# Hybrid decoder layer: norm chain, order and held splits between the output projection and the FFN, order of attention tiles, and a new table of weave distances

## The chip, the cores and the metric

The kernel runs on one core of a Trainium2 chip. The metric is the device time of one execution in microseconds (us), the median over several runs. In the profile PE is TensorE's matmul stream, PEld its weight loads, DVE is VectorE, ACT is ScalarE, POOL is GpSimd and SP is SyncE, which here only issues DMAs (SPq). The granted TensorE clock is 1.00 at full speed and 0.50 at half.

## The reference, cut to what matters

One layer on 1024 tokens of width 1024, in float32:

```python
h = rms_norm(x, norm_mix_pre)
z = h @ w_in                            # q, k, v of attention; r, k, v and low-rank columns of RWKV-7
attn = rms_norm(dilated_attention(q, k, v), attn_out_gain)
rw = rwkv7(...)                         # 8 heads, state 64x64, a recurrence over the tokens
mixed = concat([attn, rw], -1) @ w_out
x = x + rms_norm(mixed, norm_mix_post)
h = rms_norm(x, norm_ffn_pre)
f = square(relu(h @ w_ffn_up)) @ w_ffn_down
x = x + rms_norm(f, norm_ffn_post)
# rms_norm(x, g) = x * rsqrt(mean(x*x) + 1e-6) * g
```

## The kernel before, in words

Every large product is made of three matmuls (`mm3`, L59): each operand is split into a high part (fp32r, an ACT copy) and a low part (DVE: value minus high part), and high x high, low x high and high x low are added up in PSUM. So each operand costs one ACT and one DVE instruction before PE can use it.

**The weave (to about 435 us).** The input projection is cut into slabs of 128 columns; each slab is 2 x 8 filler pieces of three matmuls. Between them the RWKV work is woven in by a planner, `drive`. It has a list of jobs, each a generator that issues some instructions and then yields the PE time it took and the time until its next step may come. The planner keeps its own clock: it takes the first job in the list that is due, adds its PE time, and if none is due it takes one filler piece (0.7). The due times stand in the table `WAIT` (L31): `'ab1.0'` is the time after the first step of job `ab1`, `'e0'` the time before job `e0` starts, and keys such as `PE7`, `EO7_0`, `VU7`, `T7` and `H7` times after particular marks. Inside the planner PE and SP keep this written order; ACT and DVE are ordered by Tile's scheduler by priority. For each unit n of 128 tokens there are the jobs `ld` (its loads AR and K), `zl` (its load Zp), `vu`, `ab` (products with a mask; T1, T2 come out), `e` (E, from Zp and T2), `c` (the recurrence: `c.0` and `c.2` multiply T1 with HV, `c.1` and `c.3` T2 with VU) and `g` (gate, norm, store). T2 lies in two tiles TR0 and TR1 for even and odd units. The slabs aq3, ak3 and av3 come after the last unit; 28 of their pieces are issued ahead of the attention (`LEAD`).

**Attention.** `at_load` (L869 to L880) loads for a pair of heads the tiles qs, kh and kl of each head, 12 DMAs on SP, and `at_s`, `at_t` and `at_v` make scores, transposes and outputs. These tiles lie in a pool that is opened over the space of pools closed before: places are handed out in the order in which the tiles are created, and a load into a place waits until the last user of what lay there is through.

**Output projection to FFN (about 610 to 730 us).** For tiles of 128 tokens in the order 0, 4, 1, 5, 2, 6, 3, 7 `half_mm` (L1002) multiplies half of the mixed row with half of `w_out`: 24 matmuls into two PSUM banks `pm`. `mix_x1` (L1009 to L1037) makes both norms and the residual of one tile on ACT and DVE: squares of pm, the root (`rstd1`, L97 to L106), y = pm * rstd * gain (L1028), y + x (L1029), the store to `x_d`, a square of y (L1032), the second root, and the scaled tile `yg` (L1035 on DVE, L1036 on ACT). `mix_h2` (L1039) transposes `yg` on PE and makes from it, for token half 0, high and low parts HB and raw copies, and for half 1 the combinations T1 to T4. From here PE's order is the order in which the program is written.

The FFN's two products are done with a Strassen-like scheme of seven products on halves. Up: for each of 16 groups j, `up_first` (L1218) makes two products X and Y from a split weight W1, `first_out` evacuates them, and `up_last` makes five more (X with T2, Z with T1, X with T3, Z with HB, X with T4) from the splits W2, W3 and W4 of `up_rest` (L1197). Before the last tile was ready, groups 0 and 1 had their `up_first`; group 2 had it directly after the last tile's transposes. `split_w` (L1185 to L1190) is the split of a weight. The results are spilled to DRAM (`u_d`), and the down product reads them back. The last norm, `final` (L1408), uses `rstd1` too.

`rstd1` was: ACT root s of the mean, DVE v = -mean/2, y = 1/s, then a Newton step, y * (1.5 + v * y * y), in three steps.

Of the kernel before, what the change touches and what calls it, by code (L numbers as in the profile page):

```python
# [1 line left out]

# [38 lines left out]
def hybrid_kernel(tc, x, par, cst, strip, win, wup_lora, gup, gnwb, grow, wout, wup, wdown, out, dbg=None):  # L41
# [22 lines left out]
    with (  # L64
# [10 lines left out]
        eps = cp.tile([P, 32], F32, name="eps")[:, 0:1]  # L75
# [18 lines left out]
        eps1 = cp.tile([P, 1], F32, name="eps1")  # L94
        A.activation(eps1, eps, AF.Sqrt)

        def rstd1(y, ssum, nm, more=eps, more_v=-0.5 * NORM_EPS):  # L97
# [6 lines left out]
            V.tensor_tensor(m, y, y, OP.mult)  # L104
            V.tensor_tensor(m, m, v_, OP.mult)
            V.scalar_tensor_tensor(y, m, 1.5, y, OP.add, OP.mult)  # L106
# [762 lines left out]
        def at_load(p):  # L869

            at[p] = QS, KH, KL = [], [], []
            for h in range(2):
                hs_ = slice(64 * h, 64 * h + 64)
                for L, nm, q, js in ((QS, "qs", p, (0, 1)), (KH, "kh", 4 + p, (0, 0)), (KL, "kl", 4 + p, (1, 1))):
                    t = aset[p % 2].tile([P, S], F32R, name=f"{nm}{p}_{h}", tag=f"{nm}{h}", bufs=1)
                    for d in range(2):
                        nc.sync.dma_start(t[own[d]].bitcast(F32), qk_d[q, js[d], hs_, :])
# [124 lines left out]
        def half_mm(t, pm, mx, k0, first, last):  # L1002
            for n in range(2):
                ns = slice(n * 512, n * 512 + 512)
                for k in range(4):
                    w = WO[k0 + k]
                    mm3(pm[n], mx[:, 0, k], mx[:, 1, k], w[:, 0, ns], w[:, 1, ns], first and k == 0, last and k == 3)

        def mix_x1(t, pm, y=None):  # L1009
# [12 lines left out]
            for n in range(2):  # L1022
                A.activation(jm, src[n], AF.Square, accum_out=st[:, 2 + n:3 + n])
            V.tensor_tensor(st[:, 2:3], st[:, 2:3], st[:, 3:4], OP.add)
            rstd1(st[:, 4:5], st[:, 2:3], f"m{t}")
            for n in range(2):
                ns = slice(n * 512, n * 512 + 512)
                V.scalar_tensor_tensor(y[:, ns], src[n], st[:, 4:5], gpM[:, ns], OP.mult, OP.mult)  # L1028
# [6 lines left out]
            V.tensor_tensor(yg, y, gF, OP.mult)  # L1035
            A.activation(yg, yg, AF.Copy, scale=st[:, 6:7])  # L1036
            return yg  # L1037

        def mix_h2(t, yg, between=None):  # L1039
# [9 lines left out]
            for q in range(h, 2):  # L1049
                A.activation(HB[q, h][:, 0, :, qs], pt[q], AF.Copy)  # L1050
            if h == 0:
                for q in range(2):
                    A.activation(f((T3, T4)[q]), pt[q], AF.Copy)
                    last = V.tensor_tensor(HB[q, 0][:, 1, :, qs], pt[q], HB[q, 0].bitcast(F32)[:, 0, :, qs], OP.subtract)  # L1054
                return last
# [105 lines left out]
        pms[1] = pm_new(ORD[1], "bc")  # L1161
        for i in range(8):
# [21 lines left out]

        def split_w(raw, nm, E=V, pool=None):  # L1185
# [3 lines left out]
            E.tensor_tensor(w[:, 1, 0:n], raw, w[:, 0, 0:n].bitcast(F32), OP.subtract)  # L1189
# [7 lines left out]
        def up_rest(j, r1, r2):  # L1197
# [340 lines left out]
```

## Time and profile before

| what | value |
|---|---|
| median of 3 runs | 1333.93 us (1330.68 to 1336.93) |
| the profiled execution's own time | 1336.02 us |
| its span, first to last instruction | 1334.2 us |
| mean granted TensorE clock | 0.987 |
| DVE busy | 900.3 us, 67% |
| ACT busy | 629.0 us, 47% |
| POOL busy | 40.9 us, 3% |
| DMA | 240.57 MB, mean 180 GB/s |
| chain that ended last, by engine | PE 68%, DVE 12%, DMA 11%, ACT 5% |

The span is what the trace shows of one execution; the execution's own time is 1.8 us longer. Lines such as L1036 are lines of the kernel before. A row of the timeline has start, length, engine, line, operation, output and inputs, shapes and a count; in brackets stands the idle time before it on its engine and what ended it. Matmuls overlap, so the start of the next one tells more than the length. Most matmuls have L47, the helper `mm`, and are told apart by their tiles.

### The profile page before, as it was taken

To read this page: it belongs to the slowest core of one execution; us is meant where nothing else is said; L and a number is where in the kernel's file an instruction comes from. 1 tells how busy PE (TensorE), PEld (TensorE's weight loads), DVE (VectorE), ACT (ScalarE), POOL (GpSimd) and SP (SyncE) were. 2 spreads that over 40 slices of the span, in tenths; PEclk is the share of its full clock that TensorE was granted. 3 is DMA by queue.
4 is the path that set the end of the run, shared out by engine and by line. 5 is a ranking of instruction groups with operands and counts; after the bars stand their busy time and mean duration, and the time that the engine had idled before them with its cause. 6 is when DMAs were issued, how large, how long until landed. Compare 5 with 4: busy or idle time off the path is not lost.

```text
span 1334.2 us, 23879 instructions
## 1 busy us (share of the span) xinstructions
PE 1268.8 (95%) x9488; PEld 1043.3 (78%) x9488; DVE 900.3 (67%) x1648; ACT 629.0 (47%) x1033; POOL 40.9 (3%) x59
## 2 busy tenths in 40 slices
PE   6899999999988979999998999999999999999997
PEld 5678788877776867787887888888887888888885
DVE  7877678542878456555878977766766776446585
ACT  7653423232554267665746444444444444444343
POOL 0000000000000000000000000000000002000211
PEclk9999999999998989999999999999999999999998
DMA  7345767976684687403523554444457984345564
GB/s 260 112 181 158 208 156 204 279 206 193 215 264 130 200 234 199 127 25 96 174 103 118 195 169 150 138 146 174 150 195 244 369 300 147 95 142 198 194 214 151
DMA packets 168240, 240.57 MB, mean 180 GB/s; under 512 B 56672, under 2 KB 93792, under 8 KB 168128
## 3 DMA queue, kind: packets, MB, share of 16 engines
q1 hardware_dynamic: 158784, 213.86, 50.5%
q10 hardware_dynamic: 8064, 20.98, 4.8%
q0 software_dynamic: 1280, 4.20, 0.8%
q8 instruction: 75, 1.23, 0.4%
q14 instruction: 37, 0.30, 0.1%
HBM read 161.90 MB, written 77.09 MB: 179 GB/s over the span
## 4 chain that ended last, share of the span: by engine, by line
PE 68%; DVE 12%; DMA 11%; ACT 5%; issue 3%; SPq 1%; DVEq 0%; ACTq 0%
PE X L47 13%; PE dX L47 9%; PE Z L47 7%; PE pm L47 6%; PE dZ L47 5%; PE Y L47 3%; PE dY L47 3%; PE z_v L47 3%; PE z_aq L47 3%; PE z_ak L47 2%; PE pS L47 2%; PE po L47 2%; PE pT L920 2%; PE O L47 2%; PE z_r L47 1%
## 5 line engine op out<-in xcount | busy, mean ns | idle before, releaser
L47 PE MATMUL dX<-wow,wou 128*128 128x512 f32 x768 | 178.2, 393 | 2.8 <-DVE wow L1189 1.6
L47 PEld LDWEIGHTS dX<-wow,wou 128*128 128x128 f32 x768 | 144.8, 189 | 35.5 <-DVE wow L1189 3.5
L47 PE MATMUL dZ<-wow,wou 128*128 128x512 f32 x384 | 87.4, 389 | 0.0
L1188 ACT ACTIVATE wow<-wd 128x1024 fp32r<-128x1024 f32 x40 | 42.3, 1060 | 89.1 <-PE dZ L47 29.7
L47 PEld LDWEIGHTS dZ<-wow,wou 128*128 128x128 f32 x384 | 72.1, 188 | 14.9
L1189 DVE TENSOR_TENSOR wou<-ur,wou 128x1024 fp32r<-128x1024 f32 x56 | 71.7, 1282 | 9.1 <-ACT wou L1188 8.9
L1189 DVE TENSOR_TENSOR wow<-wd,wow 128x1024 fp32r<-128x1024 f32 x40 | 49.2, 1231 | 35.6 <-ACT wow L1188 35.2
L1188 ACT ACTIVATE wou<-ur 128x1024 fp32r<-128x1024 f32 x56 | 58.5, 1048 | 21.1 <-DMA ur<-u_d 13.8
L908 DVE CUSTOM_DVE_ANT_0 S<-pS,stripT 128x512 f32<-128x512 f32 (+3 forms) x64 | 37.7, 589 | 39.2 <-PE pS L47 37.6
L910 ACT ACTIVATE S<-S,mn 128x128 f32<-128x128 f32 (+7 forms) x64 | 49.3, 771 | 16.2 <-DVE mn L908 15.7
L1276 ACT ACTIVATE r<-u 128x512 f32<-128x512 f32 x48 | 30.0, 626 | 48.4 <-DVE u L1274 48.2
L920 PE MATMUL pT<-cst,S 128*128 128x128 f32 x288 | 44.4, 281 | 7.6 <-ACT PT L922 6.3
L47 PE MATMUL pm<-WO,mxr 128*128 128x512 f32 x192 | 49.2, 400 | 0.8 <-DVE mxr L988 0.8
L47 PE MATMUL X<-HB,wo 128*128 128x512 f32 x180 | 45.2, 401 | 3.9 <-DVE HB L1054 2.3
L1189 DVE TENSOR_TENSOR wow<-TK,wow 128x1024 fp32r<-128x1024 f32 x16 | 20.8, 1301 | 38.9 <-ACT wow L1188 38.9
L47 PE MATMUL Z<-HB,wo 128*128 128x512 f32 x192 | 46.1, 389 | 0.0
L47 PE MATMUL z_aq<-hT,wh_aq 128*128 128x512 f32 x128 | 46.1, 421 | 0.0
L1460 POOL TENSOR_TENSOR E<-E,gpF 128x512 f32<-128x512 f32 x12 | 21.1, 1771 | 806.3 <-DMA xf<-x_d 640.3
L47 PE MATMUL pm<-WO,mxa 128*128 128x512 f32 x192 | 45.7, 393 | 0.0
L47 PE MATMUL z_av<-hT,wh_av 128*128 128x512 f32 x128 | 44.9, 408 | 0.0
L920 PEld LDWEIGHTS pT<-cst,S 128*128 128x128 f32 x288 | 32.9, 142 | 15.3 <-ACT PT L922 11.3
L47 PE MATMUL z_k<-hT,wh_k 128*128 128x512 f32 x128 | 43.4, 396 | 1.4 <-DVE z L234 1.4
(394 smaller groups left out, 3060.7 us busy)
## 6 DMA issues: line engine op xcount, KB each, us to landing
ur<-u_d SPq DMA_DIRECT2D x56, 512.0 KB, 4.2
wd<-in_wdown_dram SPq DMA_DIRECT2D x40, 512.0 KB, 4.4
u_d<-S SPq DMA_DIRECT2D x64, 256.0 KB, 2.1
u_d<-u SPq DMA_DIRECT2D x48, 256.0 KB, 2.3
wr_upa<-in_wup_dram SPq DMA_DIRECT2D x16, 512.0 KB, 3.6
wr_upb<-in_wup_dram SPq DMA_DIRECT2D x16, 512.0 KB, 4.1
TK<-in_wdown_dram SPq DMA_DIRECT2D x16, 512.0 KB, 6.8
x<-in_x_dram SPq DMA_DIRECT2D x8, 512.0 KB, 7.1
```

What stands on the lines that cost most here:

```text
L47: return PE.matmul(o, lhsT, rhs, start=start, stop=stop, skip_group_check=True)
L908: V.tensor_tensor_reduce(Sx[:, lo:hi], pS[:, :hi - lo], stripT[:, so:so + hi - lo], 1.0, 3e38 if k == 0 else mn[:, 0:1], OP.add, OP.min, a ...
L910: A.activation(Sx[:, :w], Sx[:, :w], AF.Exp, scale=-1.0, bias=mn[:, nbk - 1:nbk], accum_out=at[p, "den"][:, i, h:h + 1])
L920: PE.transpose(pt[:, j], Sx[:, (4 * k + j) * P:(4 * k + j + 1) * P], ident)
L1188: A.activation(w[:, 0, 0:n], raw, AF.Copy)
L1189: E.tensor_tensor(w[:, 1, 0:n], raw, w[:, 0, 0:n].bitcast(F32), OP.subtract)
L1276: A.activation(r, src, AF.Relu)
L1460: G.tensor_tensor(e, e, gn[n], OP.mult)
```

## The change

- `rstd1` takes another last step (Heron): with s the root of mean/4 on ACT and v = mean/4, y = 1/(s + v/s). For one column that is a reciprocal, one fused step and a reciprocal; for two columns four steps.
- `mix_x1` multiplies pm with the gain right after the squares, without waiting for the root. After the root one fused step per half makes y * rstd + x, and ACT squares each half as it comes. The last scaling is halved between ACT and DVE.
- The transposes of tile 3 (`ORD[6]`) go into the last `half_mm`, ahead of its last six matmuls.
- Splits are held back by `issue_after`: the second early split W1[1] behind the high and low parts of tile 3, the splits of groups 2 and 3, W2 of group 0 and the T splits behind the last tile's squares and sums; some of the last tile's combinations behind W2's low part; W3 and W4 of group 0 behind T1's low part.
- Groups 2 and 3 (before: group 2) have their `up_first` before group 0's `up_last`; Y2 moves from bank w to bank a. Group 3's split lies in the tiles of `mixy`, which is closed later.
- `at_load` creates the tiles of the second head first. The order of the loads stays.
- `WAIT` has 147 entries that are new, changed or gone.

```diff
-WAIT = {..., 'mrg0.0': 31.5, 'e0': 14.5, 'ab1.0': 2, 'c1.2': 2, 'c2.0': 0, 'e3': 0, 'ab4.0': 3.5, 'c6.0': 0, 'c7.0': 8.0, 'H7': 6.0, 'PE7': 2.5, ...}
+WAIT = {..., 'mrg0.0': 28.0, 'e0': 14.0, 'ab1.0': 8, 'c1.2': 1, 'c2.0': 0.5, 'e3': 1.5, 'ab4.0': 0, 'c6.0': 0.5, 'c7.0': 2.5, 'H7': 2.5, 'PE7': 0, ...}
...
-            A.activation(sq_, ssum, AF.Sqrt, scale=1.0 / D, bias=more)
-            V.tensor_scalar(v_, ssum, -0.5 / D, more_v, op0=OP.mult, op1=OP.add)
-            V.reciprocal(y, sq_)
-            V.tensor_tensor(m, y, y, OP.mult)
-            V.tensor_tensor(m, m, v_, OP.mult)
-            V.scalar_tensor_tensor(y, m, 1.5, y, OP.add, OP.mult)
+            A.activation(sq_, ssum, AF.Sqrt, scale=0.25 / D, bias=more)
+            V.tensor_scalar(v_, ssum, 0.25 / D, more_v, op0=OP.mult, op1=OP.add)
+            V.reciprocal(m, sq_)
+            if n == 1:
+                V.scalar_tensor_tensor(m, m, v_, sq_, OP.mult, OP.add)
+            else:
+                V.tensor_tensor(m, m, v_, OP.mult)
+                V.tensor_tensor(m, m, sq_, OP.add)
+            V.reciprocal(y, m)
...
-            at[p] = QS, KH, KL = [], [], []
+            T = {(nm, h): aset[p % 2].tile([P, S], F32R, name=f"{nm}{p}_{h}", tag=f"{nm}{h}", bufs=1) for h in (1, 0) for nm in ("qs", "kh", "kl")}
...
+        BK = 2
...
+                    if between and (n, k) == (1, BK):
+                        between()
...
+            for n in range(2):
+                V.tensor_tensor(y[:, hs[n]], src[n], gpM[:, hs[n]], OP.mult)
             V.tensor_tensor(st[:, 2:3], st[:, 2:3], st[:, 3:4], OP.add)
             rstd1(st[:, 4:5], st[:, 2:3], f"m{t}")
...
-                V.scalar_tensor_tensor(y[:, ns], src[n], st[:, 4:5], gpM[:, ns], OP.mult, OP.mult)
-            V.tensor_tensor(y, y, xt, OP.add)
+                ld = V.scalar_tensor_tensor(y[:, hs[n]], y[:, hs[n]], st[:, 4:5], xt[:, hs[n]], OP.mult, OP.add)
+                la = A.activation(jh[:, hs[n]], y[:, hs[n]], AF.Square, accum_out=st[:, (5, 7)[n]:(6, 8)[n]])
...
-            A.activation(yg, yg, AF.Copy, scale=st[:, 6:7])
+            A.activation(yg[:, hs[0]], yg[:, hs[0]], AF.Copy, scale=st[:, 6:7])
+            V.tensor_scalar(yg[:, hs[1]], yg[:, hs[1]], st[:, 6:7], None, op0=OP.mult)
...
-            half_mm(ORD[i], pms[i], ax.pop(i), 0, i < 2, True)
+            half_mm(ORD[i], pms[i], ax.pop(i), 0, i < 2, True, last_h0 if i == 7 else None)
...
-        for j in range(2):
-            W1[j] = split_w(up_raw(2 * j, f"e{j}"), f"1_{j}")
-        h6 = mix_h2(ORD[6], ygs.pop(6))
+        W1[0] = split_w(up_raw(0, "e0"), "1_0")
+        with tc.issue_after(h6s[0][0].ins), tc.issue_after(h6s[0][1].ins):
+            W1[1] = split_w(up_raw(2, "e1"), "1_1")
...
+        with tc.issue_after(ea.ins), tc.issue_after(ed.ins):
+            W1[2] = [stg.tile([P, D], F32R, name=f"w12{q}", tag=("wh", "wl")[q]) for q in range(2)]
...
+            W1[3] = [M["yp"].tile([P, D], F32R, name=f"w13{q}", tag="y") for q in range(2)]
...
+            ws0 = up_rest(0, up_raw(0, "a0"), up_raw(1, "b0"), True)
+            for k, v in TS.items():
+                A.activation(v[1][:, :, early_], v[0][:, :, early_], AF.Copy)
...
+            for j in (2, 3):
+                with tc.high_priority(offset=20):
+                    c11s[j - 2] = first_out(j - 2)
+                up_first(j, W1[j])
...
-                elif j < 3:
+                elif j < 4:
```

More of the change, by code (lines that the diff above doesn't have):

```diff
@@ L1 @@
+import contextlib
 import math
+import contextlib
 import numpy as np
@@ L1000, in half_a, with half_mm @@
             return half_t(t, m, "a", tag)
-        def half_mm(t, pm, mx, k0, first, last):
+        BK = 2
+        MX = {}
+        def half_mm(t, pm, mx, k0, first, last, between=None):
             for n in range(2):
@@ L1049, in mix_h2 @@
             for q in range(h, 2):
-                A.activation(HB[q, h][:, 0, :, qs], pt[q], AF.Copy)
+                la = A.activation(HB[q, h][:, 0, :, qs], pt[q], AF.Copy)
             if h == 0:
                 for q in range(2):
-                    A.activation(f((T3, T4)[q]), pt[q], AF.Copy)
                     last = V.tensor_tensor(HB[q, 0][:, 1, :, qs], pt[q], HB[q, 0].bitcast(F32)[:, 0, :, qs], OP.subtract)
-                return last
+                with tc.issue_after(la.ins):
+                    for q in range(2):
+                        A.activation(f((T3, T4)[q]), pt[q], AF.Copy)
+                return la, last
             V.tensor_tensor(f(T1), pt[0], f(T3), OP.subtract)
@@ L1059, in mix_h2 @@
                 between()
-            V.tensor_tensor(HB[1, 1][:, 1, :, qs], pt[1], HB[1, 1].bitcast(F32)[:, 0, :, qs], OP.subtract)
-            V.tensor_tensor(f(T3), f(T2), f(T3), OP.subtract)
-            V.tensor_tensor(f(T4), f(T4), f(T2), OP.subtract)
+            with (tc.issue_after(W2I[0].ins) if between else contextlib.nullcontext()):
+                V.tensor_tensor(HB[1, 1][:, 1, :, qs], pt[1], HB[1, 1].bitcast(F32)[:, 0, :, qs], OP.subtract)
+                V.tensor_tensor(f(T3), f(T2), f(T3), OP.subtract)
+                V.tensor_tensor(f(T4), f(T4), f(T2), OP.subtract)
         def pm_new(t, tags):
@@ L1188, in split_w @@
             A.activation(w[:, 0, 0:n], raw, AF.Copy)
-            E.tensor_tensor(w[:, 1, 0:n], raw, w[:, 0, 0:n].bitcast(F32), OP.subtract)
+            low = E.tensor_tensor(w[:, 1, 0:n], raw, w[:, 0, 0:n].bitcast(F32), OP.subtract)
+            if nm == "2_0":
+                W2I.append(low)
             return w
@@ L1221, in up_first @@
             prod(XB[j], op2(w, 0), HQ[0, 0], True)
-            y = bank(f"Y{j}", "w" if j == 2 else YT[j % 2])
+            y = bank(f"Y{j}", YT[j % 2])
             prod(y, op2(w, 1), HQ[1, 0], True)
@@ L1255, in t2_late @@
             t_low(2, late, V)
-        mix_h2(ORD[7], ygs.pop(7), t2_late)
-        up_first(2, W1[2])
-        for k in (1, 3, 4):
-            A.activation(TS[k][1][:, :, late], TS[k][0][:, :, late], AF.Copy)
-            new_low(k)
-            t_low(k, slice(0, 512), V)
-        HT = {k: v[1:] for k, v in TS.items()}
+        with tc.high_priority(offset=PRI[0]):
+            mix_h2(ORD[7], ygs.pop(7), t2_late)
         mix_ctx.__exit__(None, None, None)
-        M["yc"].__exit__(None, None, None)
         if "x1" in dbg:
@@ L1314, in up_last @@
                     spill(i, j, t)
-            c11s = {j: first_out(j) for j in range(2)}
+            c11s = {}
+            for j in (2, 3):
+                with tc.high_priority(offset=20):
+                    c11s[j - 2] = first_out(j - 2)
+                up_first(j, W1[j])
+            for k in (1, 3, 4):
+                A.activation(TS[k][1][:, :, late], TS[k][0][:, :, late], AF.Copy)
+                new_low(k)
+                if k == 1:
+                    with tc.high_priority(offset=PRI[1]):
+                        t1l = t_low(k, slice(0, 512), V)
+                    with tc.issue_after(t1l.ins):
+                        ws0 = ws0()
+                else:
+                    t_low(k, slice(0, 512), V)
+            HT = {k: v[1:] for k, v in TS.items()}
             for j in range(NPR):
```

75 lines of the change are left out of this document (43 added, 32 removed).

## The prediction

> **What bounds the kernel now.** I read the page first, then the busy time by stretches, then PE's timeline with the waits in brackets, then ACT, DVE and the DMA queue of SP around those waits. The first two lines are the page's; the others are stretches: PE busy, PEld busy, DVE busy, ACT busy, POOL busy, then the granted TensorE clock, DMA share and GB/s.
>
> ```profile
> span 1334.2 us, 23879 instructions
> PE 1268.8 (95%) x9488; PEld 1043.3 (78%) x9488; DVE 900.3 (67%) x1648; ACT 629.0 (47%) x1033; POOL 40.9 (3%) x59
> 750.00:800.00 50.00, 50.00 (x222) 41.44 (x221) 40.22 (x59) 21.83 (x32) 0.00 (x0) 1.00 0.54 188
> 316.60:320.00 3.40, 3.40 (x16) 2.23 (x12) 0.00 (x0) 1.19 (x2) 0.00 (x0) 0.50 0.89 169
> 425.80:435.50 9.70, 7.40 (x113) 6.61 (x109) 7.08 (x20) 2.87 (x5) 0.00 (x0) 0.50 0.19 65
> 435.50:439.50 4.00, 4.00 (x12) 3.14 (x11) 2.31 (x11) 1.22 (x2) 0.00 (x0) 0.50 0.59 197
> 470.20:477.03 6.83, 4.56 (x15) 3.65 (x15) 1.28 (x6) 1.28 (x6) 0.00 (x0) 0.50 0.99 336
> 709.13:712.55 3.42, 3.42 (x8) 2.66 (x9) 3.42 (x5) 3.42 (x4) 0.00 (x0) 0.50 0.49 168
> ```
>
> PE is busy for 1268.8 of 1334.2 us, and no matmul is added or taken away. So the change can gain only in two ways: fewer of the 65 idle microseconds, and fewer microseconds at half clock, where PE looks busy and does half. The stretch 750 to 800 stands for the FFN: PE full, full clock, nothing to win. The four places at clock 0.50 each follow a wait, so a wait costs more than its own length. I price that as half of PE's busy time there: 1.7 at 316.6, 5.7 at 425.8 to 439.5 (half of 7.40 + 4.00), 2.3 at 470.2, 1.7 at 709.1.
>
> **The transition from output projection to FFN.** PE in order of time (start, length, then what; brackets: idle before and its releaser), and one piece of the chain that ended last, for the price of an undisturbed group of 12:
>
> ```profile
> 697.86 5.71 PE L47 MATMUL pm<-WO,mxa 128*128 128x512 f32 x24
> 703.40 1.04 PE L1048 MATMUL h2t<-cst,yg 128*128 128x128 f32 x8
> 706.03 0.73 PE L47 MATMUL X<-HB,wo 128*128 128x512 f32 x2 [1.60 <-ACT HB L1050]
> 709.04 4.14 PE L47 MATMUL X<-HB,wo 128*128 128x512 f32 x10 [2.27 <-DVE HB L1054]
> 713.02 2.90 PE L47 MATMUL Y<-HB,wo 128*128 128x512 f32 x12
> 715.92 2.72 PE X L47 x12
> ```
>
> From 703.40 to 713.02 PE does eight transposes and 12 matmuls in 9.62 us. Undisturbed these are some 0.9 (the transposes, without the pipelined end) and 2.72, together 3.6. So 6.0 us are lost: 1.60 + 2.27 of waiting and the rest to the clock. What released them, ACT and then DVE:
>
> ```profile
> 701.46 1.14 ACT L1036 ACTIVATE yg<-yg,st 128x1024 f32<-128x1024 f32 x1
> 702.50 1.04 ACT L1188 ACTIVATE wo<-wr_upe 128x1024 fp32r<-128x1024 f32 x1
> 703.45 1.47 ACT L1237 ACTIVATE T2h<-T 128x1536 fp32r<-128x1536 f32 x1
> 704.82 0.58 ACT L1023 ACTIVATE jm<-pm 128x512 bf16<-128x512 f32 x1
> 705.39 0.59 ACT L1050 ACTIVATE HB<-h2t 128x512 fp32r<-128x512 f32 x1
> 715.69 1.16 ACT L1036 ACTIVATE yg<-yg,st 128x1024 f32<-128x1024 f32 x1
> 697.62 1.22 DVE L1035 TENSOR_TENSOR yg<-y,gF 128x1024 f32<-128x1024 f32 x1
> 706.98 1.41 DVE L1028 SCALAR_TENSOR_TENSOR y<-pm,st,gpM 128x512 f32<-128x512 f32 x2
> 708.31 0.68 DVE L1054 TENSOR_TENSOR HB<-h2t,HB 128x512 fp32r<-128x512 f32 x1
> 727.61 2.28 DVE L1241 TENSOR_TENSOR T1l<-T,T1h 128x2048 fp32r<-128x2048 f32 x1
> 1328.86 0.16 DVE L104 TENSOR_TENSOR r1m_f<-stF 128x1 f32<-128x1 f32 x1
> ```
>
> The transposed tile stood in PSUM at about 704.3, but ACT ran a split (1.04), a T split (1.47) and a square (0.58) ahead of its copy at 705.39, and DVE ran the last tile's norm (1.41) ahead of the low part at 708.31. The last two rows price a whole low part and one small step of a norm chain.
>
> **The change part by part.**
>
> *Transposes inside the last half product.* They go ahead of matmul 19 of 24: 18/24 of the way from 697.86 to 703.40 is 702.0. They end at 702.9, and six matmuls (1.36) cover until 704.2. ACT's high part then starts at 702.9 and ends at 703.5; DVE's low part (0.68) ends at 704.2, and X's third matmul, the first to read it, comes at 704.7. So no wait is left if nothing stands ahead, and the holds see to that: the second early split now follows the transposes' copies, and the T splits follow the last tile's squares. The scaled tile must exist by 702.0; before it was ready at 702.6. After the first root the new chain has one half of the multiply-add (0.70) and one half-width square before the second squares can overlap, in place of 1.41 + 1.22 and a full square (about the 1.04 of a copy of that width): over 1.5 us earlier. I take 0.5 of the 6.0 lost as remaining: **-5.5**. Ends: -6.0, and -3.9 if the clock part stays.
>
> *The last tile (needed by PE's second set of transposes).* PE reaches them at 704.2 + four products of 2.72 = 715.1. Before, the tile was scaled at 715.69 + 1.16 = 716.9, with three T splits in between on ACT. Those go behind it now and the chain is shorter, so I expect it before 712: cost 0 under 10.9 us of products; without the holds it would be 1.7 late.
>
> *Four groups ahead.* Two products (5.4 us) of group 3 move forward; nothing is added. What is due next is T1's low part, for the second product of group 0. From 704.2 PE has four pairs (21.8), transposes (0.9) and one product (2.72): 25.4 us. DVE has, in that time: the last tile 0.70 + 1.41 + 1.22 + 0.68 and eight small steps at 0.16 (5.3); four splits at 1.22 (4.9); sums of raw weights 4 x 0.68 (2.7); T2's low part, 2.28 by width plus recombination 2 x 0.68 (3.7); two evacuations of two steps (2.7); T1's low part (2.28); the low part and recombinations held until W2's split, 3 x 0.68 (2.0). Sum 23.6. It fits with 1.8 us to spare, hence 0; the held W3 and W4 splits (1.22 + 0.68) come after, where their products are one and three later. In groups 2 and 3 DVE has about 13.3 us (12 steps of 0.68 of evacuation, sums and small split, 5.1 of the rest) against five products, 13.6: 0 to +2, taken as **+0.5** for all of it. PSUM holds: Y2 moves to bank a, free after the first evacuation, 5.4 us before it is needed.
>
> *Heron root.* One small step fewer for single columns, the same count for two columns, so nothing at the start. At the end three such chains lie one behind the other after the last matmuls, each one step of 0.16 shorter: **-0.5**. In the middle it is hidden by PE.
>
> *Attention tiles, second head first.* PE, then SP's own issues, and from the view of the tile kl the time its loads take to land:
>
> ```profile
> 433.55 1.97 PE L47 MATMUL O<-VU,TR 128*64 128x64 f32 x32 [0.68 <-ACT VU L646]
> 448.11 0.39 PE L47 MATMUL z_aq<-hT,wh_aq 128*128 128x512 f32 x1
> 470.29 0.44 PE L47 MATMUL pS<-kh,qs 128*128 128x128 f32 x1 [1.75 <-DMA kh<-qk_d]
> 472.91 0.47 PE L47 MATMUL pS<-kl,qs 128*128 128x128 f32 x1 [2.18 <-DMA kl<-qk_d]
> 452.71 1.10 SPq L877 DMA_DIRECT2D qs<-qk_d  x2
> 459.09 1.38 SPq L877 DMA_DIRECT2D qs<-qk_d  x2
> 467.38 1.08 SPq L877 DMA_DIRECT2D kl<-qk_d  x2
> DMA to landing us min/median/max: 4.0/6.8/8.6
> ```
>
> The loads still go first head first; only the places change. By the order of creation, the strip and then six tiles lie upward over the space that the evacuation slots and the two TR tiles left. The first tile of the six lies on evacuation slots, which the aq3 projection uses until after 448.11; that is why the first load goes at 452.71 and holds everything behind it on SP. Now the second head lies there, and the first head lies on TR, whose last reader ends at 435.5. So the first head's six loads and the strip can go from about 436, and the second head's six at 452.7 instead of 459 to 468. By the issue lengths (1.1 to 1.4 for two) they are out by about 457, and even at 8.6 each they land by 466, before PE comes at 467.4. That removes 1.75 + 2.18 and the 2.3 of clock; about 1 comes back, as the softmax chain then is what PE waits for. **-5.0**, from -6.2 to 0 if SP still holds the first load.
>
> *Weave distances.* 147 entries differ. I worked the planner's arithmetic (first number of each yield onto its clock, due times from the table) through for both tables; for before it gives exactly the order of matmuls in the trace. The new order has no new work, and nearly every step moves by one to five filler pieces of 0.7 us; SP's queue moves with it. Four of the old waits, and SP's queue ahead of the first:
>
> ```profile
> 315.99 1.43 PE L47 MATMUL E<-TR,Zp 64*64 64x128 f32 x16 [2.49 <-DMA Zp<-zp_d]
> 351.94 1.15 PE L47 MATMUL O<-VU,TR 128*64 128x64 f32 x32 [0.69 <-ACT VU L646]
> 374.98 1.09 PE L47 MATMUL E<-TR,Zp 64*64 64x128 f32 x16 [2.27 <-ACT TR L584]
> 413.70 1.15 PE L47 MATMUL O<-VU,TR 128*64 128x64 f32 x32 [0.83 <-ACT VU L646]
> 299.29 0.32 SPq L560 DMA_DIRECT2D AR<-ar_d  x1
> 310.59 1.25 SPq L567 DMA_DIRECT2D Zp<-zp_d  x2
> SPq L625 <- DMA qk_d<-evh_ak: 6.3, 1, 6.3
> ```
>
> Zp: with ab1.0 from 2 to 8 unit 3's loads (299.29) go behind Zp's. Ahead of Zp's loads SP stood 6.3 us at a load of VU for an unrelated transfer; two loads fewer ahead change which transfer each has to wait for. I take half of 2.49 + 1.7: -2.1 (ends -4.2 and +2). E4's second half: ab4.0 from 3.5 to 0 puts ab4.1 ahead of c3.1, two more filler pieces and 1.1 lie between it and its reader: -2.0 of 2.27. Pairs that stood side by side: c2.0 and c2.1 now have e3.0 between them, c6.0 and c6.1 a filler: -1.3 of 0.69 + 0.83. Against it: e3.0 comes 3 us earlier than before and reads what ACT writes, filler is taken from between c1.2 and c1.3, and the loads meet other transfers: +1.4, with 0 and +12 as ends (6.3 as SP's wait above, 5.7 as the longest half clock). Sum **-4.0**.
>
> In all -5.5 + 0.5 - 0.5 - 5.0 - 4.0 = **-14.5**. The profiled execution took 1336.0 (span 1334.2 and 1.8 around it), so 1321.5. It lies 2.1 above the median of the runs shown, 1333.9; I forecast the median as 1320.
>
> **A rule against it.** The trace shows half clock from 709.13 after two waits of 1.60 and 2.27. The Trainium skill, TensorE: Matmul & The Clock Gate, section "HAM oscillation — how this bites in real kernels", states the rule as no PE-idle gaps over about 3.4 us. By that rule these waits would not cost clock; here the trace speaks otherwise, as both are shorter.
>
> **The rivals.**
> 1. The half-clock stretches come from something else and stay when the waits go: 2.3 (attention), 1.7 (transition) and about half of 1.7 (Zp) are not gained, 1325. Against: each dip begins within a microsecond of a listed wait. The rule above would put it here. Chance 0.06.
> 2. The weave takes the gain back: one more wait on SP of the kind that cost 6.3, late, where no filler is left, with 5.7 of half clock, and no gain from the 4.0: 1336. For: 425.8 to 439.5 shows the price. 0.14.
> 3. The first head's loads stay behind SP's other work, 5.0 not gained: 1325. 0.08.
> 4. Slower: two such waits ahead of the loads of units 5 to 7, each 6.3 + 5.7. That is +24 with the -4.0 lost: 1348. It decides once the weave loses over 17 us, since the other parts bring 10.5. Against: the planner's tail is the same work in nearly the same order. 0.07.
> 5. The weave loses all four quoted waits and its long half clock, another -8: 1312. 0.05.
> DVE as the bound in groups 0 to 3 is inside the forecast's own range; at 2 us late in each of two groups it costs 4.
>
> **How the numbers follow.** Forecast 0.60, its own range 1311 to 1327. Half a percent of 1333.9 is 6.7, about what a measurement of this kernel can tell from no change: faster below 1327.2, slower above 1340.6. Faster: 0.60 less 0.03 of its tail, rival 1, rival 5 and 0.05 of rival 3, 0.73. Same: rival 2 and the remainders, 0.20. Slower: 0.07. The range 1308 to 1335 leaves out rival 4, half of rival 2 and the end of rival 5.
>
> **What would show it.** Transition: transposes inside the last pm group, X following pm with under 1 us idle and no 0.50 near 709. Attention: first qs load near 436 on SP, no wait for kh or kl. Weave: E without a wait for Zp, half clock at 425 perhaps still there. Tail: three small DVE steps after the root instead of four. The forecast is wrong if the idle time of PE between 100 and 440 grows, or if X or Z waits for DVE after 715.

## The result, and the profile after

The changed kernel takes 1323.6 us (median of 12 runs, 1317.5 to 1334.6) against 1336.55 for the kernel before on the same chip (1329.09 to 1344.94): a ratio of 0.9901, 95% interval 0.9874 to 0.9928. Forecast were 1320 us and faster, with a range of 1308 to 1335. The total came out as forecast; the terms behind it did not all do so, and that is the subject here.

The page of after, its span and its engines:

```profile
span 1322.5 us, 23897 instructions
PE 1267.4 (96%) x9488; PEld 1042.7 (79%) x9488; DVE 903.6 (68%) x1645; ACT 626.9 (47%) x1049; POOL 41.0 (3%) x59
```

PE is as busy as before (1268.8), and the idle time fell from 65.4 to 55.1 us. Line numbers below are each kernel's own. PE at the transition, the answer to the rows from 697.86 to 715.92 in the prediction:

```profile
695.61 1.03 PE L1064 MATMUL h2t<-cst,yg 128*128 128x128 f32 x8
696.40 1.62 PE L49 MATMUL pm<-WO,mxa 128*128 128x512 f32 x6
697.86 2.88 PE L49 MATMUL X<-HB,wo 128*128 128x512 f32 x12
700.58 2.88 PE L49 MATMUL Y<-HB,wo 128*128 128x512 f32 x12
708.74 1.04 PE L1064 MATMUL h2t<-cst,yg 128*128 128x128 f32 x8
709.54 3.01 PE L49 MATMUL X<-HB,w 128*128 128x512 f32 x12
712.83 3.06 PE L49 MATMUL Y<-HB,w 128*128 128x512 f32 x12 [0.28 <-DVE u L1306]
718.78 3.04 PE L49 MATMUL Y<-HB,w 128*128 128x512 f32 x12 [0.17 <-DVE u L1306]
```

The transposes lie inside the last product, X follows with no wait, and no half clock comes near. But Y of groups 2 and 3 now waits for DVE. At the start of attention, first PE, then SP's own issues, then the longest of SP's waits (in total, times, longest):

```profile
461.82 0.33 PE L49 MATMUL pS<-kh,qs 128*128 128x128 f32 x1 [0.48 <-DVE mn L916]
463.45 0.30 PE L49 MATMUL pS<-kl,qs 128*128 128x128 f32 x1 [1.31 <-DMA kl<-qk_d]
```

```profile
439.28 0.32 SPq L692 DMA_DIRECT2D r_d<-Y  x1
441.41 1.10 SPq L886 DMA_DIRECT2D qs<-qk_d  x2
447.54 1.08 SPq L886 DMA_DIRECT2D qs<-qk_d  x2
448.81 8.57 SPq L886 DMA_DIRECT2D kh<-qk_d  x2
457.42 1.24 SPq L886 DMA_DIRECT2D kl<-qk_d  x2
```

```profile
SPq L886 <- DMA qk_d<-evh_ak: 7.7, 1, 7.7
```

The first load goes at 441.41, not near 436, and the second head's kh takes SP 8.57 us, because its second issue stands 7.7 us for a store of ACT (evh_ak). The wait of PE fell from 1.75 + 2.18 to 1.31. The half-clock windows of after, by stretches (columns as in the prediction):

```profile
272.70:276.10 3.40, 3.40 (x34) 2.87 (x24) 1.78 (x3) 0.60 (x1) 0.30 (x1) 0.50 0.28 92
392.15:395.55 3.40, 3.40 (x41) 2.54 (x39) 1.66 (x6) 1.09 (x3) 0.00 (x0) 0.50 0.92 184
426.30:433.13 6.83, 6.30 (x42) 5.27 (x43) 5.76 (x20) 1.70 (x3) 0.00 (x0) 0.50 0.34 115
463.80:467.20 3.40, 3.40 (x13) 2.67 (x12) 0.99 (x4) 0.71 (x4) 0.00 (x0) 0.50 1.03 421
480.90:484.30 3.40, 3.38 (x14) 3.09 (x14) 2.58 (x6) 2.09 (x4) 0.00 (x0) 0.50 1.05 257
614.00:617.41 3.41, 3.41 (x12) 2.73 (x11) 0.69 (x1) 1.39 (x3) 0.00 (x0) 0.50 0.39 117
697.80:721.60 23.80, 23.35 (x105) 18.70 (x105) 22.65 (x37) 19.11 (x30) 0.00 (x0) 1.00 0.44 144
```

The long window at the weave's end is half as long (6.83 for 13.7), those at 316.6 and 709 are gone, and those at 272.7, 392.2, 480.9 and 614 are new. Apart from the end of the span, half clock adds up to 23.9 us, for 27.3 before. The last row shows DVE busy for 22.65 of 23.80 us where the four groups run.

To compare stages rather than totals I measured every profiled execution, of the kernels and the experiments, between the same matmuls: the weave (first z_k to the last O's end), attention (first pS to last po), the second half of the output projection (first pm of mxa to first Y), the FFN's up products (first Y to last X). Times in us; "POOL" means that the high parts of aq3 and ak3 are stored by POOL.

| kernel | table, transition | median | ratio to before (95%) | weave | attention | pm to Y | Y to last X |
|---|---|---|---|---|---|---|---|
| before | old, old | 1336.6 | 1 | 395.1 | 145.1 | 91.0 | 302.6 |
| e3_tiles | old, old | 1334.4 | 0.9988 (0.9969 to 1.0007) | 391.1 | 145.4 | 91.8 | 303.3 |
| e11_before_pool, POOL | old, old | 1332.9 | 0.9967 (0.9939 to 0.9996) | 385.5 | 144.2 | 90.9 | 302.6 |
| e12_before_mrwo | old, old | 1346.6 | 1.0072 (1.0042 to 1.0101) | 391.1 | 157.2 | 92.6 | 303.4 |
| e1_transition | old, new | 1333.4 | 0.9984 (0.9957 to 1.0011) | 393.1 | 146.4 | 87.3 | 305.1 |
| e2_weave | new, old | 1327.7 | 0.9910 (0.9878 to 0.9942) | 392.1 | 141.6 | 92.4 | 302.6 |
| after | new, new | 1323.6 | 0.9901 (0.9874 to 0.9928) | 389.5 | 143.8 | 86.3 | 304.9 |
| e5_no_holds | new, no holds | 1325.3 | 0.9918 (0.9893 to 0.9943) | 392.8 | 142.3 | 87.7 | 308.0 |
| e6_three_groups | new, 3 groups | 1319.3 | 0.9867 (0.9823 to 0.9911) | 388.7 | 142.1 | 86.3 | 306.5 |
| e7_old_root | new, new | 1324.8 | one run | 392.0 | 143.8 | 86.3 | 305.8 |
| e8_after_product | new, transposes late | 1322.2 | one run | 386.1 | 143.3 | 87.1 | 307.0 |
| e4_spill_pool, POOL | new, new | 1320.5 | 0.9882 (0.9853 to 0.9910) | 395.2 | 141.0 | 86.1 | 304.4 |
| e9_evac_first, POOL | new, new | 1319.9 | 0.9879 (0.9846 to 0.9912) | 390.3 | 141.6 | 86.1 | 304.5 |
| e10_pool_old_tiles, POOL | new, new | 1320.5 | 0.9878 (0.9835 to 0.9921) | 391.2 | 140.3 | 85.9 | 305.2 |

The column of the weave is the warning in this table: with the new table of distances the same order of matmuls takes 386.1 to 395.2 us from one profiled execution to the next, as waits and half-clock windows fall. A few microseconds there between two traces say nothing; between kernels that do not differ there, the other columns repeat within about 2 us.

### The profile page after: what moved, and what is told of

Its sections match the earlier page's. It is cut to its first block, busy times and chain, and to the rows that moved or that the text cites. A ratio compares the mean times of both kernels' runs of the same rounds, so it can differ in the third digit from the quotient of the medians.

```text
span 1322.5 us, 23897 instructions
## 1 busy us (share of the span) xinstructions
PE 1267.4 (96%) x9488; PEld 1042.7 (79%) x9488; DVE 903.6 (68%) x1645; ACT 626.9 (47%) x1049; POOL 41.0 (3%) x59
## 4 chain that ended last, share of the span: by engine, by line
PE 72%; DVE 11%; DMA 9%; ACT 4%; issue 2%; SPq 1%; DVEq 0%; ACTq 0%
PE X L49 12%; PE dX L49 8%; PE pm L49 6%; PE Z L49 6%; PE dZ L49 5%; PE z_v L49 3%; PE dY L49 3%; PE z_aq L49 3%; PE Y L49 3%; PE z_r L49 2%; PE pT L928 2%; PE pS L49 2%; PE po L49 2%; PE O L49 2%; PE z_ak L49 2%
## 5 line engine op out<-in xcount | busy, mean ns | idle before, releaser
L916 DVE CUSTOM_DVE_ANT_0 S<-pS,stripT 128x512 f32<-128x512 f32 (+3 forms) x64 | 37.6, 588 | 35.0 <-PE pS L49 31.1
L928 PEld LDWEIGHTS pT<-cst,S 128*128 128x128 f32 x288 | 33.7, 144 | 14.7 <-ACT PT L930 10.8
L49 PE MATMUL dY<-wow,wou 128*128 128x512 f32 x192 | 43.7, 389 | 0.0
```

The source lines that it names most:

```text
L49: return PE.matmul(o, lhsT, rhs, start=start, stop=stop, skip_group_check=True)
L916: V.tensor_tensor_reduce(Sx[:, lo:hi], pS[:, :hi - lo], stripT[:, so:so + hi - lo], 1.0, 3e38 if k == 0 else mn[:, 0:1], OP.add, OP.min, a ...
L928: PE.transpose(pt[:, j], Sx[:, (4 * k + j) * P:(4 * k + j + 1) * P], ident)
```

## The experiments

Theory A is the prediction: each part works locally by its own mechanism. The rivals change with the part and are named with each run.

**One part at a time: e1_transition, e2_weave, e3_tiles.**

```
e1  after,  WAIT = the old table; tiles made "for h in (0, 1)"
e2  before, WAIT = the new table
e3  before, at_load as in after (tiles made "for h in (1, 0)")
```

> The changed kernel with the old table of distances and the old tile order: only norm chain, Heron root, held splits, transposes in the last half product and four groups ahead. Theory A (each part acts where it stands, and what it saves stays saved): X starts without a wait and without half clock, first Y about 6.0 us earlier than in the kernel before relative to the first product of the attention half; about 1 to 2.3 us of that given back by DVE in the groups; tail 0.5 to 0.7 earlier. In all 4 to 5 us faster, ratio 0.996 to 0.997. Rival B (the table alone makes the gain, what the transition saves is given back in the groups): within 1 us of before.

> The kernel before with the new table of distances alone. Theory A: the same order of steps as in the changed kernel, so no wait for Zp at the first E, no 2.27 wait at E4's second half; last O product 5 to 6 us earlier, and the attention starts as much earlier; 5 us faster in all, ratio 0.996. Rival B: 10 us or more, ratio 0.992. Rival C: the loads of the attention land no earlier, so the earlier end turns into a wait at kh and kl, 1 to 2 us faster.

> The kernel before with the attention tiles created second head first, alone. The forecast's theory (places decide when the loads may start): first qs load near 436 on SP, no wait for kh and kl, 5 us faster. Theory A (the first load waits for the writes of qk_d that stand before it, and a later load for an unrelated write that uses the same DMA semaphore): first qs load not before 441, a wait of 1 us or more is left in front of the second head's scores, 0 to 2 us faster.

e1: from pm to first Y 3.7 us less, with 2.5 us given back by the last X; the total, 0.9984, can't be told from no change, nor from the 0.996 to 0.997 expected. e2: 0.9910, most of the whole gain; that is rival B's 0.992 and not the 0.996 of theory A. e3: nothing. Its own queue of SP, with the wo load ahead of it:

```profile
447.45 0.33 SPq L956 DMA_DIRECT2D wo<-in_wout_dram  x1
448.69 1.10 SPq L877 DMA_DIRECT2D qs<-qk_d  x2
464.55 1.08 SPq L877 DMA_DIRECT2D kl<-qk_d  x2
```

First head's tiles now lie on TR, whose last reader ends at 431.5 there, and still the first load goes at 448.69, 14.7 us ahead of the first pS as in before. The place was not what held it.

**What holds the loads: e4_spill_pool, e10_pool_old_tiles, e11_before_pool, e12_before_mrwo.** Rival B: a load of SP stands for an unrelated store of ACT, with which it shares a completion semaphore, which the program gives out in turn to the DMAs of both. Rival C: the first load waits for the stores to qk_d that stand ahead of it in the scheduled program. Rival D: it stands behind the mr and wo loads in SP's queue.

```
e4   after:  -A.dma_start(qk_d[..0..], zh)  +(G if i in (15, 19) else A).dma_start(...)
e10  e4 with the tiles made "for h in (0, 1)"
e11  before with the line of e4
e12  before: the loads of mr and wo  -nc.sync.dma_start  +G.dma_start
```

> The changed kernel, but the high parts of aq3 and ak3 are stored by POOL's queue instead of ACT's. Theory A (SP's second load of kh stands 8 us because the semaphore it is given was last used by the store of ak3's high part): SP issues the twelve loads without that stand, no wait for kl on PE (1.31) and no half clock near 464 (1.7): 2 to 3 us faster than the changed kernel. Rival: the load waits for its data or for transfer bandwidth; then kl still lands at the same time and the run is within 1 us of the changed kernel.

> The kernel after with the high parts of aq3 and ak3 stored by POOL, and with the attention tiles in the old order, first head first. The theory that a load of SP stands for the last user of its semaphore says that the places do not matter once no store of ACT is in the ring: the first load of qs at 446 to 450 on SP and the six loads of each head without a stand over 2.5 us, the attention stage (first pS to last po) within 1 us of the run with POOL and the new order, 1319 to 1323 in all. The theory of the places says that the second head's loads come 6 us later than with the new order and PE waits 2 to 4 us for them, 1323 to 1327.

> The kernel before with one edit: the high parts of aq3 and ak3 are stored by POOL in place of ACT. If the second head's last loads stood for ACT's store of ak3 through a shared semaphore (4.2 us in before's DMA queue of SP), they go out 3 to 4 us earlier, PE's waits of 1.75 and 2.18 us for kh and kl go, and with them the half clock of 6.8 us: 4 to 6 us less between first pS and last po, 1330 to 1333 in all. If the loads are late for their places, the waits stay within 0.5 us and the time is before's.

> The kernel before with two kinds of loads issued by POOL in place of SP: mr (the rows of r_d) and wo (the rows of the output weights). In the four runs with the old table one of each stands on SP between the last store of Y and the first attention load, which goes 14.7 us before the first pS; in the six with the new table they come behind the loads, which go 18 to 18.8 us before it. If SP's queue holds the loads, the first load of qs goes 2 to 3 us after the last r_d store, at least 17.5 us ahead of the first pS, and the stretch from first pS to last po falls from 145 us to 141 to 143 with the old table and the old places. If the loads wait for data that the old table delivers late, the lead stays at 14.7 and the stretch at 145.

In e4 SP no longer stands; its rows for the second head, against 448.81 8.57 in after:

```profile
452.50 1.16 SPq L886 DMA_DIRECT2D qs<-qk_d  x2
453.70 1.24 SPq L886 DMA_DIRECT2D kh<-qk_d  x2
456.82 1.64 SPq L886 DMA_DIRECT2D kl<-qk_d  x2
```

In after the held issue of kh goes at 456.94, 0.02 us after ACT's store of ak3 (issued at 448.08) has landed, and the trace gives both the same semaphore. In e4 PE's wait of 1.31 for kl and the half-clock window at 463.8 are gone too.

Attention takes 141.0, 141.6 and 140.3 in the three kernels with POOL and the new table, against 141.6 to 143.8 (mean 142.8) in the six without: B is worth about 1.9 us. e10, with the old places, is the shortest of all: the order of the places does nothing. In e11 the stand goes too, but my 4 to 6 us were a miss: attention loses 0.9, and PE still waits 1.57 and 1.73 for kh and kl. PE came to attention sooner after the loads' start than with the new table: 14.7 us from the first load to the first pS, as in before.

That lead is the key. It is 14.7 in before, e3, e1 and e11 and 17.9 to 18.8 in every kernel with the new table. What sits at its start is a store. POOL in before, then in after (both halves of aq3's low part):

```profile
444.71 0.54 POOL L716 DMA_DIRECT2D qk_d<-evl_aq  x1 [66.97 <-DVE evl_aq L714]
450.15 0.54 POOL L716 DMA_DIRECT2D qk_d<-evl_aq  x1 [4.90 <-DVE evl_aq L714]
```

```profile
438.19 0.54 POOL L725 DMA_DIRECT2D qk_d<-evl_aq  x1 [67.19 <-DVE evl_aq L723]
443.63 0.54 POOL L725 DMA_DIRECT2D qk_d<-evl_aq  x1 [4.90 <-DVE evl_aq L723]
```

In before the first qs load (452.71) goes after the second store, 450.15. In after (441.41) it goes after the first, 438.19, and ahead of the second. So it is in all kernels: with the old table 2.5 to 3.4 us behind the second half, with the new one 3.2 to 3.3 behind the first. The load reads rows of aq0, stored long before. By rival C it waits for aq3's store because that stands ahead of it. e12 was to tell C from D. It is slower by 12 us in attention (waits of PE of 2.70, 2.38, 3.09 and 1.66), with mr and wo among POOL's stores; which of these did it I did not follow up. The queue of SP in e12, without mr and wo, and its wait there:

```profile
441.12 0.32 SPq L683 DMA_DIRECT2D r_d<-Y  x1
448.87 1.10 SPq L877 DMA_DIRECT2D qs<-qk_d  x2
```

```profile
SPq L877 <- DMA qk_d<-evh_aq: 4.8, 1, 4.8
```

With nothing between them, the load still goes 7.75 us after r_d's store, waiting 4.8 for a store of aq3, and leads the first pS by 13.8. So it is C that ends the wait: in all five kernels with the old table the load goes 0.1 to 0.3 us after the second half of aq3's low part has landed (452.40 in before), and in e11 no store of ACT is among them. D stood close behind: wo is issued at 451.48 in before, ahead of the load, so without C the load could have come at most 0.9 us sooner. The new table orders both behind the loads, and that gives 3 to 4 us of lead. What lands last ahead of the first load is then r_d's last store (issued at 439.28 in after, landed at 441.27, 0.1 to 0.2 us before the load in all nine kernels); why the load waits for that one is not shown.

**The transition: e5_no_holds, e8_after_product, e6_three_groups, e9_evac_first.**

```
e5  after without its five "with tc.issue_after(...)"
e8  after: half_mm(..., last_h0 if i == 7 else None)  ->  half_mm(...); if i == 7: last_h0()
e6  after: W1[3] and up_first(3) back in the loop over groups
e9  e4 and first_out under high_priority(offset=400) in place of 20
```

> The kernel after with the five holds taken away (the second early split no longer waits for the transposes' copies, the early splits of groups 2 and 3, group 0's weights and the T splits no longer wait for the last tile's squares, the recombination copies and the rest of W2's group wait for nothing); everything else as after. If the holds carry the gain at the transition, the low part that X reads third comes behind two whole splits (2 x 1.2 us) on DVE, X waits 1.5 to 2.5 us, and a stretch of half clock of 3.4 us may follow: first Y 2 to 4 us later against the last output-projection matmul than in the kernel after, 1325 to 1328 in all. If the place of the transposes inside the last product carries it, the wait at X stays below 0.5 us and the time is the kernel after's, 1322 to 1325.

> The kernel after with the transposes of the seventh tile behind the last half product in place of inside it; holds and chain as after. PE then stands between the transposes and X for ACT's high part and DVE's low part: 0.6 + 0.6 us after the transposes' end, 1 to 1.5 us from the last pm to first Y, with or without a stretch of half clock of 3.4 us (another 1.7). If the chain alone were the gain, X would start within 0.3 us of the transposes and no more than 0.3 us would be lost.

> The kernel after with the products of only three groups ahead: group 3's early split and its X and Y go back to where before had them. If the fourth group is what crowds DVE (Y waits, the later wait of 0.69 us for T4), the stretch from first Y to the last X loses 1 to 2 us against after's 304.9: 303 to 304. If the crowding comes from the last tile's norm and the holds, which both have, it stays at 304.5 to 305.5. The total cannot show either; 1322 to 1326.

> The kernel after with two edits: the high parts of aq3 and ak3 are stored by POOL in place of ACT, and the first evacuations of groups 0 and 1 have so high a priority that DVE takes them ahead of the weight sums and the recombination. If DVE's order is what makes Y of groups 2 and 3 wait (0.28 and 0.17 us after), these waits go and the stretch from first Y to X of T2, 21.07 us after, becomes 20.5; if the 1.1 us over eight undisturbed pieces are issue and the end of the transposes, it stays at 21.0. The stand of SP at the second head's loads is gone as in the earlier run with POOL. In all 1319 to 1323.

PE in e5, then in e8:

```profile
699.64 2.56 PE L49 MATMUL X<-HB,wo 128*128 128x512 f32 x10 [0.83 <-DVE HB L1069]
715.88 4.57 PE L49 MATMUL Y<-HB,w 128*128 128x512 f32 x12 [1.90 <-DVE u L1306]
```

```profile
690.91 1.04 PE L1064 MATMUL h2t<-cst,yg 128*128 128x128 f32 x8
692.40 3.40 PE L49 MATMUL X<-HB,wo 128*128 128x512 f32 x12 [0.45 <-ACT HB L1066]
695.64 2.88 PE L49 MATMUL Y<-HB,wo 128*128 128x512 f32 x12
708.67 3.02 PE L49 MATMUL Y<-HB,w 128*128 128x512 f32 x12 [1.09 <-DVE u L1308]
```

Without the holds X waits 0.83 and the last pm is 4.22 us from first Y (2.95 in after); then Y waits 1.90 and runs at half clock (4.57 for 2.88), so that the first product with T2 starts 23.8 us after first Y, not 21.1. The holds carry 1.3 + 2.7 us locally, less than I expected at X and more behind it. In e8 PE needs 4.73 us from the transposes to Y where 0.8 + 2.72 are undisturbed: 1.2 lost, as expected, without half clock. By the table's column e8 loses 0.8 (87.1 for 86.3). So the place inside the product is worth some 1 of the 6.0, in one run, and chain and holds the rest.

e6 refutes my suspicion of the fourth group: Y to last X gets longer (306.5), since PE comes to T3's low part five microseconds earlier and waits 2.13 us for it:

```profile
719.77 0.50 PE L49 MATMUL X<-T3l,wo 128*128 128x512 f32 x1 [2.13 <-DVE T3l L1266]
```

The fourth group is cover, not load. (e6's low median, 1319.3, does not come from here; its interval overlaps after's.)

e9 removes the waits of Y. What stood ahead of the first evacuation (L1306) on DVE in after, and a later wait of X there:

```profile
709.69 0.68 DVE L1227 TENSOR_TENSOR s<-wr_upb 128x512 f32<-128x512 f32 x1
710.30 0.68 DVE L1074 TENSOR_TENSOR T<-h2t,T 128x512 f32<-128x512 f32 x1
710.90 0.68 DVE L1228 TENSOR_TENSOR s<-s,wr_upa 128x512 f32<-128x512 f32 x1
711.50 0.68 DVE L1075 TENSOR_TENSOR T<-h2t,T 128x512 f32<-128x512 f32 x1
712.10 0.68 DVE L1306 TENSOR_TENSOR u<-Y,s 128x512 f32<-128x512 f32 x1
793.44 0.73 PE L49 MATMUL X<-T4h,wo 128*128 128x512 f32 x2 [0.69 <-DVE u L1306]
```

PE and DVE in e9:

```profile
708.40 3.03 PE L49 MATMUL Y<-HB,w 128*128 128x512 f32 x12
713.99 2.88 PE L49 MATMUL Y<-HB,w 128*128 128x512 f32 x12
716.71 0.61 PE L49 MATMUL X<-T2h,wo 128*128 128x512 f32 x2
```

```profile
707.66 1.28 DVE L1306 TENSOR_TENSOR u<-Y,s 128x512 f32<-128x512 f32 x2
```

From first Y to the first product with T2 it takes 20.1 us for after's 21.1, better than the 20.5 expected. It is lost again further on, where X waits 0.66 (at 755.61) and 0.41 (at 788.99) for DVE: to the last X e9 takes 304.5 us, and e4, which differs from it by the priority alone, 304.4.

**The root: e7_old_root.**

```
e7  after with before's rstd1 and its st[:, t, 5:6] in final
```

> The kernel after with the old root (one Newton step on the reciprocal of the square root). The forecast put 0.5 us on three chains of one small step each at the end: the stretch from the last dX to the end of the span 0.3 to 0.6 us longer than after's 7.05, nothing at the transition, where PE hides it. If the reciprocal costs as much as the steps that it replaces, 7.0 to 7.2.

The end is as forecast: 7.54 us from the last dX to the end of the span, 7.01 in after. The start was not forecast at all. PE at 30 us, in before and in e7 (in after there is no wait at this place):

```profile
30.80 0.47 PE L47 MATMUL z_L<-hT,wh_L 128*128 128x512 f32 x1 [0.94 <-DVE zl L203]
```

```profile
30.73 0.47 PE L49 MATMUL z_L<-hT,wh_L 128*128 128x512 f32 x1 [0.94 <-DVE zl L209]
```

DVE's order there changes with the root; in after it computes zl ahead of two casts and a piece of hT that come before it in e7, at 28.32 for 29.86:

```profile
28.32 0.74 DVE L212 SCALAR_TENSOR_TENSOR zl<-z_L,par,zl 128x511 f32<-128x511 f32 x1
```

With the new root z_k starts at 39.3 to 39.9 in seven of eight kernels and at 40.5 in one whose first input came 0.8 later; with the old one at 40.4 to 40.8.

## Why the prediction was right, and which of its steps were wrong

**The direction and the size of the total** were right (1323.6 for 1320). Five points lie behind it. Of the two signs of error that the prediction names, one came: PE's idle time between 100 and 440 did not grow (17.8 to 13.8 us), but X waits for DVE after 715 (0.69 at 793.44).

- *Transition, -5.5.* Right. Between pm and first Y the five kernels without it have 90.9 to 92.6 (mean 91.7), the seven with all of it 85.9 to 87.3 (mean 86.3): -5.4. If the shares add up, the place has some 1 of it (e8) and the holds 1.3 (e5). The other 3 are left to the shorter chain, but no run takes the chain alone away; the root has no part in it (86.3 in e7).
- *Four groups and DVE, +0.5.* Mis-sized: Y to last X has a mean of 302.9 without, 305.1 with four groups at after's priorities, +2.2, just beyond its bound of +2. The step that failed is "Y2 moves to bank a, free after the first evacuation, 5.4 us before it is needed". The sum of DVE's work was fair (22.65 busy of 23.80). But the first evacuation stood in DVE's order behind sums of raw weights and recombinations and came at 712.10, so that Y2 waited 0.28 for it; e9 shows it by moving it. That step does not carry the whole miss: in e9 the waits of Y are gone and the stage is no shorter (304.5 for e4's 304.4). In after 1.14 us are waits that the profile shows (0.28, 0.17, and 0.69 for T4 at 793.44); the cause of the rest stays open.
- *Attention tiles, -5.0.* Wrong mechanism. The failed step is "the first head lies on TR, whose last reader ends at 435.5. So the first head's six loads and the strip can go from about 436". e3 has the new places and neither earlier loads nor a gain; e10 has the old ones and the shortest attention. The loads wait for stores, and the gain that came at this place, 145.6 to 142.8 on the mean (-2.8), comes from the table. The second head's early loads ran into the stand of 7.7 us, which I had read in before (4.2 us for evh_ak) only as lateness.
- *Weave, -4.0.* The size is borne out by an estimate, the single terms are not. By time the table brings 0.9910 (0.9878 to 0.9942), about 12 us of 1336.6 (8.1 between the medians, 1335.8 for before on that chip), the largest part of the change. In the profiles the weave itself seems to gain nothing: the five with the old table have a mean of 391.2, the nine with the new one 390.9. But the profiled executions are no fair sample. That of e11 is the fastest of its 12, 8.1 below the median, and that of e4 the slowest of its 6, 6.2 above. If each profile's distance from its kernel's median is taken off its weave, the five come to 392.4 to 395.6 (mean 394.2), and the seven with the new table and more than one run to 388.4 to 391.1 (mean 389.4): -4.8. This is an estimate, since it puts the whole distance into the weave. Which entries bring it stays open: Zp's wait and three others went, yet new ones came (1.94 at 271.74, 1.79 at 382.61). Besides, the table brings attention (-2.8) and the way there, from the last O to the first pS (31.1 to 29.9, -1.2, with fewer long windows at half clock at the weave's end). In all that is 8.8 of the 8 to 12.
- *Heron root, -0.5.* Right at the end (0.5), wrong with "nothing at the start": about 1.0 there.

The stages thus add up to -5.4 + 2.2 - 2.8 - 1.2 - 4.8 - 1.5 = -13.5, for -13.0 between the medians. That the total came so near is in part luck: the -5.0 was forecast for places that do nothing, and the table brought -4.0 around that spot by another mechanism; and the root's unforeseen 1.0 made up for part of the DVE term (+2.2 for +0.5). Of the rivals, the third (loads behind SP's other work) was nearest for what the places did, though the cause was a store; the second and the fourth did not come.

**The clock.** The reading that each half-clock window follows a wait held, with waits as short as 1.31 us at 463.45, and 0.90 and 0.52 (390.37 and 391.87) ahead of the window at 392.15. The Trainium skill, TensorE: Matmul & The Clock Gate, section "HAM oscillation — how this bites in real kernels", allows gaps up to about 3.4 us; the runs here disagree, as every window in the rows of after above follows shorter ones (1.71 at 425.00 ahead of the longest). But a wait is not enough: before has 1.14 + 1.50 at the very place (619.45 and 621.61) where after has 1.74 + 1.50 (611.59 and 613.75), and no window there, while e10 has 1.14 + 1.50 too, and a window from 609.75. So half a window is no fixed price for a wait, and the -5.0 and -4.0 that counted it so were loose by that. The price of a window did hold: take off each of the 14 weaves its idle time of PE and half of PE's busy time at half clock, and 385.5 to 395.2 us become 364.8 to 366.0. And "each dip begins within a microsecond of a listed wait" is not so for the longest one: the listed waits nearest to 425.8 are at 413.70 and 433.55, and what came ahead of it in before was this:

```profile
423.83 0.34 PE L47 MATMUL O<-HV,T 128*64 128x64 f32 x4 [1.08 <-DVE HV L653]
```

**The best kernel of the study** is after with the stores of aq3 and ak3 on POOL, with or without e9's priority: 1319.9 to 1320.5 in three kernels, ratios 0.9878 to 0.9882 for after's 0.9901. Each interval overlaps after's; three of three on the same side and the shorter attention speak for it, no more. e6's median is lower still (1319.3, four runs), but no stage of its profile gives a reason.

## What to carry to other kernels

When a load is late, find out which earlier transfer it waits for before counting from the memory that it fills: list, over several variants, which store it always follows. Fitting the sum of an engine's work into a window isn't enough, as a result that frees a buffer can stand late in its order; but measure the whole stage after moving it, since here 1.2 us gained in one place were lost further on. And where the same order of work scatters by several microseconds between executions, compare stages over many runs, and look where each profiled execution lies among the runs of its kernel, since a term read from one pair of traces can be chance.

## What the runs showed of the hardware

- A DMA of SP can stand for an unrelated one of ACT: 4.2 us in before, 7.7 in after, gone in the four kernels where POOL stores instead (e4, e9, e10, e11).
- Half-clock windows, but for those at the end of the span, have lengths of 3.4 us and its multiples (6.8, 10.2, 13.7). They can follow waits of under 2 us (1.31 at 463.45 in after), but not every such wait has one: the same 1.14 + 1.50 have a window in e10 and none in before.
- A weave with the same order of matmuls takes 386.1 to 395.2 us (nine profiles); idle time and half of the busy time at half clock account for all of the differences but 0.9.
- Vector steps of 0.68 us by the profile start 0.60 apart on DVE when they stand back to back (709.69 to 712.10 in after): sums of such durations, as in the prediction, come out over 10% too long.
